# A hybrid mixer with PEER experts: one mixer for all 512 tokens, and U products ahead of the V products

## The chip, the cores and the metric

The kernel runs on one core of a Trainium2 chip. The metric is device microseconds of one execution. Engines: TensorE (PE; PEld is its weight load), VectorE (DVE), ScalarE (ACT), GpSimd (POOL), and SyncE (SP), which issues most DMAs.

## The reference, cut to what matters

512 tokens of width 1024, and 16 learned meta tokens in front of them that are dropped at the end; one layer:

```python
def hybrid_mixer(hn, w_in, w_gate_up, b_gate_up, sb_norm_g, gla_norm_g, w_out):
    proj = hn @ w_in
    ...
    sb_o = stick_breaking_attention(split_heads(sbq, SB_HEADS), split_heads(sbk, SB_HEADS),
                                    split_heads(sbv, SB_HEADS))
    ...
    return jnp.concatenate([sb_o, gla_o], axis=-1) @ w_out
```

Stick-breaking attention has 8 heads of 64: a query weighs a key by sigmoid(z) times the product of (1 − sigmoid) of the later keys, which is a softplus, a sum over keys from the right, and an exp. Beside it stand 4 heads of gated linear attention (GLA), with a decay per key dimension. x + mixer is normed, and goes through PEER: each of 8 heads picks 16 of 128 × 128 experts by product keys (top 16 of each of two lists of 128 scores, then the top 16 of their sums). The output of a token is the sum over its 128 experts of gate · gelu(x · U[e]) · V[e], where U and V are tables of 16384 × 1024 in fp32 (64 MB each). A last residual and a last norm follow.

## The kernel before, in words

The 512 tokens are four blocks of 128. For blocks 0 to 2 the experts are computed densely: the table is walked in 128 rows of 128 experts. A **U row** loads 128 experts of U (512 KB), splits them into a high and a low fp32r part (`hilo`, uh on ScalarE, ul on VectorE), and multiplies them with the normed tokens xDh, xDl (384 columns) in three passes (`mm3`, L187 to L189), which gives a PSUM tile pj, and gelu of it in SBUF. A **V row** loads 128 experts of V (vf, vh, vl), multiplies the gelu tile with the gates gt (L986), splits that into wh and wl, and adds 18 passes of 512 columns to six PSUM banks acc. The gates come from DRAM: top-k gives each token's experts and gates, and `spread` turns them into a dense matrix (one-hot B on VectorE L872, Am on GpSimd L874, matmul L878, stored as Gd; gt are loads of eight rows of it). Block 3 is computed sparsely: 128 gathers of U rows by indirect DMA from GpSimd (L820), a dot product each on VectorE (gu, L827), then 128 gathers of V rows and as many weighted sums (y, L838).

Before, the mixer runs in two groups. Blocks 0 to 2 and the meta tokens go first, in three-pass products. Then block 3 follows in native fp32 (L209), written as generators that a string interleaves by hand with the top-k and the spreads of blocks 0 to 2 and with a few U rows:

```python
SCHED = "f f f u1 f f t0 c1 f f f f m s0 t1 c2 s1 u1 u1 t2 s2 m c3"
```

Here f and m advance block 3's mixer and its second half, t and c the top-k of a block, s its spread, and u a U row. Then U rows run 23 ahead of the V rows in a ring of 24 SBUF tiles, and the main loop goes over 128 steps, each a U row, a V row, and first a share of block 3's top-k, then 2.35 gathers (`GRATE`). Every engine works through its own instructions in program order.

Of the kernel before, what the change touches and what calls it, by code (L numbers as in the profile page):

```python
# [21 lines left out]
D = 1024  # L22
# [7 lines left out]
WF = 2  # L30
GB = 5

SCT = ("px", "pz", "pz", "px")


ORDER = ("nqaylvorx", "nlvorxqay")

GRATE = 2.35
TRATE = 16


SCHED = "f f f u1 f f t0 c1 f f f f m s0 t1 c2 s1 u1 u1 t2 s2 m c3"
# [11 lines left out]
GROUPS = ((0, 1, 2), (3,))  # L54
DENSE = (0, 1, 2)
GATHER = (3,)
ND = len(DENSE)
TT = 16
TB = ND * 128 // TT
IC = 8  # L60

NATIVE_IN = (False, True)
NATIVE_OUT = (False, True)
NATIVE_PQ = (False, True)


def build(tc, d, out):
# [21 lines left out]
    nbuf = dict(pz=3, po=3)  # L89
# [13 lines left out]
    def pk():  # L103
        return bank("pk")

    A.preload_act_table_set(LNEXP)
    Gd = drp.tile([TB, 128, 128, TT], F32, name="Gd")
    hd = drp.tile([4, 128, D], F32, name="hd")

# [26 lines left out]
    def consts_b():  # L136
        nc.sync.dma_start(wgu, d["wgu"])
        nc.sync.dma_start(bgu, d["bgu"])
        lvf = pp.tile([128, 8, 128], F32, name="kT0")
# [51 lines left out]
    def proj(src, c, jobs, act, native, cols=256, halves=(0, 1)):  # L191


        for half in halves:
            wf = wp.tile([128, 4, 256], F32, name="wf", bufs=WF)
            nc.sync.dma_start(wf[:, :, :cols], src[c, :, half * 4:half * 4 + 4, :cols])
            if not native:
                wh = wp.tile([128, 4, 256], F32R, name="wh", bufs=2)
                wl = wp.tile([128, 4, 256], F32R, name="wl", bufs=2)
                hilo(wh[:, :, :cols], wl[:, :, :cols], wf[:, :, :cols])  # L200
            for (o, kind, w0, w1, t0, t1, fst) in jobs:
                for k in range(4):
                    kt = half * 4 + k
                    a = act(kt, t0, t1)
                    st, sp = kt == 0 and fst, kt == KT - 1
                    if native:
                        w = wf[:, k, w0:w1]
                        l, r = (w, a[0]) if kind == 'f' else (a[0], w)
                        T.matmul(o, l, r, start=st, stop=sp, skip_group_check=True)  # L209
                    else:  # L210
                        w = (wh[:, k, w0:w1], wl[:, k, w0:w1])
                        l, r = (w, a) if kind == 'f' else (a, w)
                        mm3(o, l, r, st, sp)

    def token_jobs(nb, lo, bank_):

        banks, outs, jobs = [], [], []
        for b in range(nb):
            if b % 2 == 0:
                banks.append(bank_())  # L220
            o = banks[-1][:, (b % 2) * 256:(b % 2 + 1) * 256]
            outs.append(o)
            jobs.append((o, 't', 0, 256, lo + b * 128, lo + (b + 1) * 128, b % 2 == 0))
        return banks, outs, jobs

    kTs, vts, oTs, qps = {}, {}, {}, {}
    win = d["w_in"]

    def front(g):

        blks = GROUPS[g]
        nb = len(blks)
        W = nb * 128
        E = NM + W
        c0 = 0 if g == 0 else NM
        nt = E - c0
        nat, nato = NATIVE_IN[g], NATIVE_OUT[g]
        pm_ = pj if g == 0 else pk
        oTh = (pp if g == 0 else wp).tile([128, KT, W], F32 if nato else F32R, name=f"oT{g}h")
        oTl = None if nato else pp.tile([128, KT, W], F32R, name=f"oT{g}l")  # L240
        oTs[g] = oTh, oTl
        es = ExitStack()
        ap = es.enter_context(tc.tile_pool(name=f"a{g}", bufs=1, reuse_waits="tile"))
        sbq = ap.tile([128, 4, W], F32, name="sbq")
        kT = (pp if g == 0 else ap).tile([128, 4, W], F32, name=f"kT{g}")
        vt = (pp if g == 0 else ap).tile([128, nb, 512], F32, name=f"v{g}")
        kTs[g], vts[g] = kT, vt
        hnh = ap.tile([128, KT, E], F32 if nat else F32R, name="hnh")
        hnl = None if nat else ap.tile([128, KT, E], F32R, name="hnl")

        tags = itertools.cycle(("pz", "po"))

        def norm_rows(x, rows):

            sq = wp.tile([128, D], F32, name="wf", bufs=WF)[:rows]
            ss = pp.tile([128, 1], F32, name="ssa", bufs=2)[:rows]
            A.activation(sq, x, AF.Square, accum_out=ss)
            r = rstd(ss, 1, rows, pp, "a")
            V.tensor_scalar(x, x, r, None, op0=OP.mult)

        def columns(x, rows, col, q):

            t = bank(next(tags)) if g == 0 else pm_()
            for k in range(4):
                T.transpose(t[:, k * rows:(k + 1) * rows], x[:, (4 * q + k) * 128:(4 * q + k + 1) * 128],
                            ident[:rows, :rows])
            for k in range(4):
                kt = 4 * q + k
                hi = hnh[:, kt, col:col + rows]
                A.activation(hi, t[:, k * rows:(k + 1) * rows], AF.Copy, scale=g1[:, kt:kt + 1])  # L270
                if not nat:
                    V.scalar_tensor_tensor(hnl[:, kt, col:col + rows], t[:, k * rows:(k + 1) * rows],
                                           g1[:, kt:kt + 1], hi.bitcast(F32), op0=OP.mult, op1=OP.subtract)

        def act(kt, a, b):
            return hnh[:, kt, a:b], None if nat else hnl[:, kt, a:b]

        def feat(c, lo):
            n = E - lo
            if 2 * n <= 512:  # L280
                p = pm_()
                outs = [p[:, :n], p[:, n:2 * n]]
            else:
                outs = [pm_()[:, :n] for _ in range(2)]
            proj(win, c, [(outs[m], 'f', m * 128, (m + 1) * 128, lo, E, m == 0 or 2 * n > 512) for m in range(2)],
                 act, nat)
            return outs

        def rows_(c, vtile, mtile):

            banks, outs, jobs = token_jobs(nb, NM, pm_)
            if g == 0:
                pm = banks[-1][:66, 256:]
                jobs.append((pm, 't', 0, 256, 0, 66, False))
            proj(win, c, jobs, act, nat)
            for b in range(0, nb, 2):
                n = min(2, nb - b)
                A.activation(vtile[:, b:b + n], banks[b // 2][:, :n * 256].rearrange("p (b c) -> p b c", b=n), AF.Copy)
            if g == 0:
                A.activation(mtile, pm[:NM], AF.Copy)  # L300

        es2 = es.enter_context(ExitStack())
        gpool = es2.enter_context(tc.tile_pool(name=f"g{g}", bufs=1, reuse_waits="tile"))
        spool = None
        if g == 0:
            spool = es.enter_context(tc.tile_pool(name=f"s{g}", bufs=1, reuse_waits="tile"))
# [5 lines left out]
        gvm = gpool.tile([NM, 512], F32, name="gvm") if g == 0 else None  # L312
        gv = gpool.tile([128, nb, 512], F32, name="gv")
        go = [gpool.tile([128, 2, nb, 128], F32, name=f"go{s}") for s in range(2)]
        gr = gpool.tile([128, 4, W], F32, name="gr")
        rbc, rgk = bc[:, :, NM:], gk[:, :, NM:]
        items = [(pr, b) for pr in range(2) for b in range(nb)]
        ch = nb if nb > 2 else 2 * nb
        pO = []
        def gla_scores():  # L320

            p = pm_()
            proj(win, 12, [(p[:66, :nt], 'f', 0, 66, c0, E, True)], act, nat, cols=66)
            A.activation(glr[:, c0:], p[:16, :nt], AF.Copy)
            for pr in range(2):
                p = pm_()
                T.matmul(p[:, :nt], wgu[:, pr * 128:(pr + 1) * 128], glr[:, c0:], start=True, stop=True)
                y = gpool.tile([128, E], F32, name="dd", bufs=2)[:, :nt]
                V.tensor_scalar(y, p[:, :nt], bgu[:, pr:pr + 1], None, op0=OP.add)
                e = gpool.tile([128, E], F32, name="qk", bufs=2)[:, :nt]  # L330
# [4 lines left out]
                cuts = ([0] if g == 0 else []) + [NM + b * 128 for b in range(nb + 1)]  # L335
                for a, b in zip(cuts[:-1], cuts[1:]):
                    V.tensor_tensor_scan(bc[:, pr, a:b], y[:, a - c0:b - c0], y[:, a - c0:b - c0], 0.0,
                                         op0=OP.add, op1=OP.bypass)

            for m, p in enumerate(feat(6, NM)):  # L340
                A.activation(gq[:, m], p, AF.Copy, scale=0.125)
            for m, p in enumerate(feat(7, c0)):
                A.activation(gk[:, m, c0:], p, AF.Copy)


            for s in range(2):
                P.memset(att[s], 0.0)

            def level(l):


                if l == 7:
                    lq, rq = rgk, gq
                else:
                    H = 1 << l
# [780 lines left out]
```

## Time and profile before

| | |
|---|---|
| time, median of 3 runs | 1720.82 us (1720.75 to 1726.9) |
| profiled execution, own time | 1722.37 us |
| its span | 1720.6 us |
| PE busy | 1608.3 us (93%) |
| DVE busy | 1233.7 us (72%) |
| ACT busy | 704.0 us (41%) |
| POOL busy | 518.2 us (30%) |
| DMA | 376.04 MB, mean 219 GB/s |

Busy times are sums over the span. A busy PE need not be at its peak, since matmuls are pipelined and their ends are modelled: the spacing of their starts is the better price. Idle time of an engine that nobody waits for costs nothing.

### The profile page before, as it was taken

Reading aid. Unit: us, or ns where it says so; the run is one execution under the profiler, and the core shown is the slowest. Engines: PE = TensorE matmul, PEld = TensorE weight load, DVE = VectorE, ACT = ScalarE, POOL = GpSimd, SP = SyncE. Lnnn points to the kernel's source line nnn. Section 1 sums busy time; section 2 is a strip of 40 time slices with the busy share of each in tenths; the row PEclk is TensorE's granted clock in tenths of the full one; section 3 lists DMA queues with packets and bytes.
Section 4 is the critical chain, followed back from the end, with each engine's and each line's share of the span. In section 5 each row is a group of like instructions: output and inputs, shape, how many; then the busy total and the mean of one; then the engine's idle time right before and its main releaser. Section 6 shows DMA issues by size and latency. Waiting matters only on the chain.

```text
span 1720.6 us, 24532 instructions
## 1 busy us (share of the span) xinstructions
PE 1608.3 (93%) x9025; PEld 1432.2 (83%) x9025; DVE 1233.7 (72%) x2484; ACT 704.0 (41%) x1104; POOL 518.2 (30%) x401
## 2 busy tenths in 40 slices
PE   6998998977888789899999999999999999999996
PEld 6957988965577788899999999999999999999875
DVE  4225747489989888978777777777777777777664
ACT  5366365314445456333333333333333333333343
POOL 0020000003345455025334344343444433444310
PEclk9999999999899899999999999999999999999998
DMA  5202125342164345689887887987888888877654
GB/s 172 81 25 86 50 80 172 110 157 102 69 233 165 123 172 203 201 274 369 308 302 283 309 308 281 317 296 289 306 301 292 303 296 299 307 280 279 210 198 133
DMA packets 145705, 376.04 MB, mean 219 GB/s; under 512 B 13712, under 2 KB 63008, under 8 KB 142512
## 3 DMA queue, kind: packets, MB, share of 16 engines
q1 hardware_dynamic: 104112, 211.92, 37.1%
q0 software_dynamic: 36864, 134.23, 21.3%
q10 hardware_dynamic: 4608, 28.31, 4.1%
q8 instruction: 71, 1.16, 0.3%
q14 instruction: 50, 0.41, 0.1%
HBM read 345.03 MB, written 29.36 MB: 218 GB/s over the span
## 4 chain that ended last, share of the span: by engine, by line
PE 79%; DVE 13%; DMA 5%; ACT 2%; issue 1%; POOL 0%; SPq 0%; DVEq 0%; ACTq 0%; POOLq 0%
PE pj L187 12%; PE pj L189 12%; PE pj L188 12%; PE acc L188 9%; PE acc L189 9%; PE acc L187 9%; PE px L878 3%; DVE B L872 2%; PE pk L209 2%; PE pz L373 1%; PE pz L539 1%; DMA vf<-expert_v 1%; PE pz L525 1%; DVE sc L788 1%; DMA wf<-w_out 1%
## 5 line engine op out<-in xcount | busy, mean ns | idle before, releaser
L189 PE MATMUL pj<-xDh,ul 128*128 128x384 f32 x1000 | 338.5, 338 | 5.9 <-DVE ul L183 5.9
L188 PE MATMUL pj<-xDl,uh 128*128 128x384 f32 x1000 | 337.9, 338 | 0.0
L187 PE MATMUL pj<-xDh,uh 128*128 128x384 f32 x1000 | 337.8, 338 | 0.0
L188 PE MATMUL acc<-vl,wh 128*128 128x512 f32 x762 | 298.7, 392 | 1.5 <-DVE vl L183 1.5
L189 PE MATMUL acc<-vh,wl 128*128 128x512 f32 x762 | 298.6, 392 | 0.0
L187 PE MATMUL acc<-vh,wh 128*128 128x512 f32 x762 | 296.3, 389 | 0.4 <-ACT vh L182 0.4
L820 POOL DMA_INDIRECT gu<-expert_u,idx x128 | 183.2, 1431 | 334.4 <-DVE gu L827 193.0
L820 POOL DMA_INDIRECT gu<-expert_v,idx x128 | 178.1, 1392 | 279.3 <-DVE y L838 203.6
L182 ACT ACTIVATE uh<-uf 128x1024 fp32r<-128x1024 f32 x125 | 132.6, 1061 | 300.2 <-PE pj L188 253.6
L874 POOL TENSOR_TENSOR Am<-ohu,ohl 128x512 f32<-128x512 f32 x96 | 129.3, 1367 | 257.0 <-PE pz L530 152.4
L183 DVE TENSOR_TENSOR ul<-uf,uh 128x1024 fp32r<-128x1024 f32 x125 | 157.9, 1263 | 56.2 <-ACT uh L182 56.2
L189 PEld LDWEIGHTS pj<-xDh,ul 128*128 128x128 f32 x1000 | 189.3, 189 | 8.3 <-DVE ul L183 8.1
L187 PEld LDWEIGHTS pj<-xDh,uh 128*128 128x128 f32 x1000 | 189.1, 189 | 4.4 <-ACT uh L182 0.2
L188 PEld LDWEIGHTS pj<-xDl,uh 128*128 128x128 f32 x1000 | 189.3, 189 | 4.1
L188 PEld LDWEIGHTS acc<-vl,wh 128*128 128x128 f32 x762 | 143.0, 188 | 30.6 <-DVE vl L183 2.7
L189 PEld LDWEIGHTS acc<-vh,wl 128*128 128x128 f32 x762 | 143.0, 188 | 29.8
L187 PEld LDWEIGHTS acc<-vh,wh 128*128 128x128 f32 x762 | 143.0, 188 | 28.6 <-ACT vh L182 1.2
L838 DVE SCALAR_TENSOR_TENSOR y<-gu,act,y 128x1024 f32<-128x1024 f32 x128 | 163.8, 1279 | 0.5
L183 DVE TENSOR_TENSOR vl<-vf,vh 128x1024 fp32r<-128x1024 f32 x127 | 154.9, 1220 | 11.2 <-ACT vh L182 11.2
L827 DVE SCALAR_TENSOR_TENSOR gu<-gu,xn 128x1024 f32<-128x1024 f32 x128 | 154.6, 1218 | 0.0
L182 ACT ACTIVATE vh<-vf 128x1024 fp32r<-128x1024 f32 x127 | 133.1, 1048 | 21.1 <-DMA vf<-expert_v 19.8
L878 PE MATMUL px<-Am,B 128*128 128x128 f32 x768 | 102.7, 283 | 26.7 <-DVE B L872 17.1
(365 smaller groups left out, 2458.2 us busy)
## 6 DMA issues: line engine op xcount, KB each, us to landing
vf<-expert_v SPq DMA_DIRECT2D x128, 512.0 KB
uf<-expert_ut SPq DMA_DIRECT2D x125, 512.0 KB
wf<-w_in SPq DMA_DIRECT2D x48, 512.0 KB
Gd<-st ACTq DMA_DIRECT2D x24, 1024.0 KB
gt<-Gd SPq DMA_DIRECT2D x16, 1536.0 KB
wf<-w_out SPq DMA_DIRECT2D x16, 512.0 KB
wf<-w_pq SPq DMA_DIRECT2D x16, 512.0 KB
h<-x SPq DMA_DIRECT2D x4, 512.0 KB
```

The costliest lines, as they stand in the source:

```text
L182: A.activation(hi, src, AF.Copy)
L183: V.tensor_tensor(lo, src, hi.bitcast(F32), op=OP.subtract)
L187: T.matmul(outp, lh, rh, start=first, stop=False, skip_group_check=True)
L188: T.matmul(outp, lh, rl, start=False, stop=False, skip_group_check=True)
L189: T.matmul(outp, ll, rh, start=False, stop=last, skip_group_check=True)
L209: T.matmul(o, l, r, start=st, stop=sp, skip_group_check=True)
L820: P.indirect_dma_start(out=u, out_offset=None, in_=d[table], in_offset=bass.IndirectOffsetOnAxis(ap=col, axis=0))
L827: V.scalar_tensor_tensor(u, u, 1.0, xns[blk], op0=OP.mult, op1=OP.mult, accum_out=acts[blk][:, k:k + 1]))
L838: V.scalar_tensor_tensor(y, u, acts[blk][:, k:k + 1], y, op0=OP.mult, op1=OP.add))
L872: V.tensor_tensor(B, io4, iT[:, 1, c_].unsqueeze(2).to_broadcast(sh), op=OP.is_equal)
L874: P.tensor_tensor(Am.rearrange("p t (u l) -> p t u l", l=8), ohu[:, l_].unsqueeze(3).to_broadcast([128, 4, 16, 8]), ohl[:, l_].unsqueeze(2 ...
L878: T.matmul(p[:, j * 128:(j + 1) * 128], B[:, j], Am[:, j], start=True, stop=True)
```

## The change

One `front` and one `mid` now serve all 512 tokens in three-pass products, with 512 moving columns. The meta tokens get matmuls of their own with 16 columns. Attention is a pipeline of three functions, with scores two steps ahead of the sums:

```diff
+        scores(0)
+        scores(1)
+        for n in range(len(steps)):
+            sticks(n)
+            if n + 2 < len(steps):
+                scores(n + 2)
+            values(n)
```

The hand-written string, the ring and the steps' rates are gone. A `Queue` runs generators by estimated costs (the number that each yield hands over): behind each U row, 4.2 × 1.3 us of top-k and spread work. U rows run in pairs, and 23 pairs are stored to DRAM (Ad) from ScalarE's queue. All top-ks and spreads end before the first V product.

```diff
-GRATE = 2.35
-TRATE = 16
...
-SCHED = "f f f u1 f f t0 c1 f f f f m s0 t1 c2 s1 u1 u1 t2 s2 m c3"
...
+WF = 3
+GB = 6
+GEB = 5
+UF = 4
...
+RATES = (1.3, 0.62)
...
+    def u_row(i1, dst):
+
+        uf = du.tile([128, KT, 128], F32, name="uf", bufs=UF)
+        uh = du.tile([128, KT, 128], F32R, name="uh", bufs=2)
+        ul = du.tile([128, KT, 128], F32R, name="ul", bufs=2)
         nc.sync.dma_start(uf, d["expert_ut"][i1])
         hilo(uh, ul, uf)
...
+    look = Queue(tks[0], spread(0), tks[1], spread(1), tks[2], spread(2), tks[3])
+    np_ = 0
+    while look.jobs and np_ < NK // 2:
+        gp = pair()
+        for i in range(2):
+            u_row(2 * np_ + i, gp[:, i])
+            look.run(4.2 * RATES[0])
+        nc.scalar.dma_start(Ad[np_], gp)
+        np_ += 1
+    look.run(1e9)
```

The dense stage takes the later 41 pairs first: their U rows are computed one pair ahead and used at once. The 23 stored pairs are read back last. Gathers of block 3 run behind U and V rows at 0.62 of the rows' time, 1.3 us counted for each, so about two per row, and are at an end after 125 U and V rows. U and V rows share the buffers uf (four), uh and ul (two each); the gathered rows have six buffers where they had five.

```diff
+    order = list(range(np_, NK // 2)) + list(range(np_))
+    pairs = {}
+
+    def fetch(p_):
+        gp = pairs[p_] = pair()
+        if p_ >= np_:
+            for i in range(2):
+                u_row(2 * p_ + i, gp[:, i])
+                rows.run(4.2 * RATES[1])
         else:
...
+            nc.sync.dma_start(gp, Ad[p_])
```

What stands on VectorE when the first top-k begins, before. The top-k's instructions (MATCH_REPLACE and MAX of sc and vv) stand among the mask copies and products of block 3's GLA (att, qk):

```order
264 L378 COPY_PREDICATED att_2855<-lvm,pz 128x256
265 L378 COPY_PREDICATED att_2856<-lvm,pz 128x256
266 L365 TENSOR_TENSOR qk<-dd,gk 128x2x64
267 L366 TENSOR_TENSOR qk<-dd,gq 128x2x64
268 L747 MATCH_REPLACE sc<-vv,sc 128x128
269 L749 MAX vv<-sc 128x8
270 L378 COPY_PREDICATED att_2855<-lvm,pz 128x256
271 L378 COPY_PREDICATED att_2856<-lvm,pz 128x256
272 L749 MAX vv<-sc 128x8 x5
```

The same place now; ul is the split of a U row:

```order
246 L638 MAX vv<-sc 128x8 x8
247 L175 TENSOR_TENSOR ul<-uf,uh 128x1024
248 L638 MAX vv<-sc 128x8 x8
249 L640 MAX_INDEX iu<-vv,sc 128x8 x8
250 L175 TENSOR_TENSOR ul<-uf,uh 128x1024
251 L640 MAX_INDEX iu<-vv,sc 128x8 x8
252 L642 MATCH_REPLACE sc<-vv,sc 128x128 x16
253 L644 MAX vv<-sc 128x8 x4
254 L175 TENSOR_TENSOR ul<-uf,uh 128x1024
```

Block 3's mixer went ahead, and a split of a U row stands after each 16 to 20 of the top-k's instructions.

The end of block 3's top-k on VectorE and the first gathered rows, now (idx are the experts' numbers, gu a gathered row and its dot, ge a gelu tile times its gates):

```order
601 L702 SCALAR_TENSOR_TENSOR idx_7052<-sel_6679 128x128
602 L175 TENSOR_TENSOR ul<-uf,uh 128x1024
603 L722 SCALAR_TENSOR_TENSOR gu,act_96<-gu,xn_3217 128x1024 x3
604 L175 TENSOR_TENSOR ul<-uf,uh 128x1024
605 L722 SCALAR_TENSOR_TENSOR gu,act_96<-gu,xn_3217 128x1024 x2
606 L841 TENSOR_TENSOR ge<-ge,gt 128x384
607 L722 SCALAR_TENSOR_TENSOR gu,act_96<-gu,xn_3217 128x1024
608 L175 TENSOR_TENSOR wl_7248<-ge,wh_7247 128x384
```

Five dots of gathered rows stand ahead of the operand of the first V row.

In the middle of the gathered V rows, VectorE before (y are the weighted sums of block 3):

```order
902 L838 SCALAR_TENSOR_TENSOR y<-gu,act_93,y 128x1024
903 L183 TENSOR_TENSOR vl<-vf,vh 128x1024
904 L838 SCALAR_TENSOR_TENSOR y<-gu,act_93,y 128x1024
905 L183 TENSOR_TENSOR ul<-uf,uh 128x1024
906 L986 TENSOR_TENSOR oT0h<-oT0h,gt 128x384
907 L183 TENSOR_TENSOR wl_8808<-v_5838,wh_8807 128x384
908 L838 SCALAR_TENSOR_TENSOR y<-gu,act_93,y 128x1024
909 L183 TENSOR_TENSOR vl<-vf,vh 128x1024
910 L838 SCALAR_TENSOR_TENSOR y<-gu,act_93,y 128x1024
```

And now:

```order
653 L733 SCALAR_TENSOR_TENSOR y<-gu,act_96,y 128x1024
654 L175 TENSOR_TENSOR wl_7839<-ge,wh_7838 128x384
655 L175 TENSOR_TENSOR ul<-uf,uh 128x1024
656 L733 SCALAR_TENSOR_TENSOR y<-gu,act_96,y 128x1024 x2
657 L175 TENSOR_TENSOR wl_7874<-ge,wh_7873 128x384
658 L175 TENSOR_TENSOR ul<-uf,uh 128x1024
659 L733 SCALAR_TENSOR_TENSOR y<-gu,act_96,y 128x1024 x3
660 L175 TENSOR_TENSOR ul<-uf,uh 128x1024
661 L733 SCALAR_TENSOR_TENSOR y<-gu,act_96,y 128x1024
```

Where one y stood per split of 1024 columns (vl or ul), about two stand now.

## Rows read from the trace of the kernel before

**Rows 1.** The page: the chain that ended last, by engine.

```profile
PE 79%; DVE 13%; DMA 5%; ACT 2%; issue 1%; POOL 0%; SPq 0%; DVEq 0%; ACTq 0%; POOLq 0%
```

**Rows 2.** Windows by stage: us, busy PE, PEld, DVE, ACT, POOL, clock, DMA, GB/s.

```profile
0.00:82.00 82.00, 67.07 (x416) 65.31 (x416) 29.29 (x72) 34.72 (x82) 2.76 (x13) 1.00 0.43 133
82.00:141.00 59.00, 58.60 (x305) 34.51 (x304) 11.96 (x18) 35.87 (x68) 13.51 (x26) 1.00 0.07 23
141.00:242.00 101.00, 96.17 (x684) 85.83 (x683) 61.20 (x116) 50.25 (x89) 0.31 (x1) 0.97 0.21 71
242.00:294.00 52.00, 46.41 (x358) 42.59 (x357) 37.32 (x69) 33.01 (x70) 0.31 (x1) 0.97 0.53 177
294.00:328.00 34.00, 34.00 (x199) 34.00 (x200) 9.81 (x13) 12.59 (x23) 0.00 (x0) 1.00 0.18 62
328.00:737.00 409.00, 338.45 (x2250) 299.05 (x2249) 369.37 (x1283) 188.43 (x278) 139.96 (x104) 0.96 0.45 157
737.00:1600.00 863.00, 863.00 (x4366) 785.80 (x4365) 641.57 (x814) 303.61 (x423) 344.66 (x244) 1.00 0.86 300
1600.00:1720.60 120.60, 104.65 (x460) 85.14 (x458) 73.18 (x102) 45.53 (x74) 16.68 (x12) 0.96 0.54 178
```

**Rows 3.** Timeline of PE, a row's first matmul each: start, us, instruction.

```profile
80.05 0.28 PE L188 MATMUL pj<-wl,hnh 128*128 128x256 f32 x1
80.17 0.28 PE L189 MATMUL pj<-wh,hnl 128*128 128x256 f32 x1
...
1002.48 0.33 PE L187 MATMUL pj<-xDh,uh 128*128 128x384 f32 x1
...
1006.66 0.39 PE L187 MATMUL acc<-vh,wh 128*128 128x512 f32 x1
...
1010.78 0.33 PE L187 MATMUL pj<-xDh,uh 128*128 128x384 f32 x1
```

**Rows 4.** Groups by line, 328 to 737 us: busy, mean ns, idle before.

```profile
L872 DVE TENSOR_TENSOR B<-io,iT 128x512 f32<-128x512 f32 x96 | 88.5, 935 | 11.4 <-PE px L878 11.2
L183 DVE TENSOR_TENSOR ul<-uf,uh 128x1024 fp32r<-128x1024 f32 x21 | 30.6, 1459 | 2.7 <-ACT uh L182 2.7
L378 DVE COPY_PREDICATED att<-lvm,pz 128x256 f32<-128x256 uint8 x16 | 6.2, 438 | 0.2
L183 DVE TENSOR_TENSOR oT0l<-kT,oT0l 128x1024 fp32r<-128x1024 f32 x3 | 3.6, 1208 | 0.0
L878 PE MATMUL px<-Am,B 128*128 128x128 f32 x768 | 102.7, 283 | 26.7 <-DVE B L872 17.1 <-issue 5.6 <-POOL Am L874 3.3
```

**Rows 5.** Timeline of DVE in the dense stage.

```profile
774.95 1.22 DVE L183 TENSOR_TENSOR ul<-uf,uh 128x1024 fp32r<-128x1024 f32 x1
776.09 0.55 DVE L986 TENSOR_TENSOR oT0h<-oT0h,gt 128x384 f32<-128x384 f32 x1
...
777.03 1.22 DVE L827 SCALAR_TENSOR_TENSOR gu<-gu,xn 128x1024 f32<-128x1024 f32 x1
...
778.17 1.22 DVE L183 TENSOR_TENSOR vl<-vf,vh 128x1024 fp32r<-128x1024 f32 x1
...
1105.55 2.60 DVE L838 SCALAR_TENSOR_TENSOR y<-gu,act,y 128x1024 f32<-128x1024 f32 x2
```

**Rows 6.** Windows in a top-k and in spreads, columns as in rows 2.

```profile
360.00:400.00 40.00, 27.92 (x213) 24.66 (x209) 38.85 (x222) 10.69 (x34) 0.00 (x0) 1.00 0.48 161
540.00:680.00 140.00, 117.14 (x823) 111.13 (x822) 123.72 (x263) 78.56 (x91) 80.45 (x59) 0.95 0.44 165
```

**Rows 7.** Timeline of POOL: gathers, idle before and its releaser in brackets.

```profile
747.39 1.10 POOL L820 DMA_INDIRECT gu<-expert_u,idx  x1 [0.31 <-issue]
...
780.81 1.68 POOL L820 DMA_INDIRECT gu<-expert_u,idx  x1 [0.60 <-DVE gu L827]
```

**Rows 8.** Windows in the first gathers, columns as in rows 2.

```profile
760.00:800.00 40.00, 40.00 (x205) 36.58 (x204) 36.34 (x56) 14.37 (x20) 18.31 (x12) 1.00 1.06 371
780.00:790.00 10.00, 10.00 (x54) 9.26 (x53) 7.67 (x13) 2.55 (x4) 4.45 (x5) 1.00 1.03 409
```

More of the change, by code (lines that the diff above doesn't have):

```diff
@@ L204, in proj @@
                     a = act(kt, t0, t1)
[L205 to L213, printed above, removed]
@@ new lines, in proj, with token_jobs @@
+                    w = (wh[:, k, w0:w1], wl[:, k, w0:w1])
+                    l, r = (w, a) if kind == 'f' else (a, w)
+                    mm3(o, l, r, kt == 0 and fst, kt == KT - 1)
+    def token_jobs(lo, banks):
+        return [(banks[b // 2][:, (b % 2) * 256:(b % 2 + 1) * 256], 't', 0, 256, lo + b * 128, lo + (b + 1) * 128,
+                 b % 2 == 0) for b in range(NB)]
+    win = d["w_in"]
+    oTh = wp.tile([128, KT, W], F32R, name="oTh")
+    oTl = wp.tile([128, KT, W], F32R, name="oTl")
@@ L257, in norm_rows @@
             A.activation(sq, x, AF.Square, accum_out=ss)
-            r = rstd(ss, 1, rows, pp, "a")
+            r = rstd(ss, 1, n, pp, "a")
             V.tensor_scalar(x, x, r, None, op0=OP.mult)
[L261 to L273, printed above, removed]
@@ L275, in act @@
-        def act(kt, a, b):
[L276 to L286, printed above, removed]
+        tags = itertools.cycle(("pz", "po", "po"))
@@ L287, in feat @@
+        consts_b()
+        def act(kt, a, b):
+            return hnh[:, kt, a:b], hnl[:, kt, a:b]
+        def feat(c, meta=None):
+            outs = [pj(), pj()]
+            jobs = [(outs[m], 'f', m * 128, (m + 1) * 128, NM, E, True) for m in range(2)]
+            if meta is not None:
+                jobs += [(meta[:, m * 16:(m + 1) * 16], 'f', m * 128, (m + 1) * 128, 0, NM, m == 0) for m in range(2)]
+            proj(win, c, jobs, act)
             return outs
         def rows_(c, vtile, mtile):
-            banks, outs, jobs = token_jobs(nb, NM, pm_)
@@ L292, in rows_ @@
[L292 to L303, printed above, removed]
@@ new lines, in values @@
+        def values(n):
+            kb, nq, nh, pr0 = steps[n]
+            for i in range(nh):
+                pr = pr0 + i
+                for b in range(kb, NB):
+                    cb_ = i * nq + (b - kb) * 128
+                    for s in range(2):
+                        hh = 2 * pr + s
+                        T.matmul(pO[b][s * 64:(s + 1) * 64, pr * 128:(pr + 1) * 128],
+                                 vt[:, kb, hh * 64:(hh + 1) * 64], as_[n][s][:, cb_:cb_ + 128],
+                                 start=(b == kb and pr == 0), stop=False, skip_group_check=True)
@@ new lines, in front @@
+        scores(0)
[5 more added lines that the diff above has]
+            values(n)
+        z = pz()
+        for pr in range(4):
+            T.matmul(z[pr * 32:(pr + 1) * 32], kbd[:, pr, :], sbq[:, pr, :], start=True, stop=False,
+                     skip_group_check=True)
+        sp = spool.tile([128, 512], F32, name="sp", bufs=4)
+        softplus(z, W, sp)
+        for hh in range(NH):
+            pr, s = divmod(hh, 2)
+            T.matmul(z, csel[:, 112 - 16 * hh:240 - 16 * hh], RS[:, s, pr], start=False, stop=False,
+                     skip_group_check=True)
@@ new lines, in front @@
+        T.matmul(z, negTb, sp, start=False, stop=True, skip_group_check=True)
+        a = spool.tile([128, 512], F32, name="a", bufs=4)
+        A.activation(a, z, AF.Exp)
+        for b in range(NB):
+            for pr in range(4):
+                T.matmul(pO[b][:, pr * 128:(pr + 1) * 128], vbd[:, pr, :], a[:, b * 128:(b + 1) * 128],
+                         start=False, stop=True, skip_group_check=True)
+        es1.close()
+        gpool = es.enter_context(tc.tile_pool(name="gla", bufs=1, reuse_waits="tile"))
@@ new lines, in build, with __init__, run @@
+    bp = pool_open("bld", "bld")
+    class Queue:
+        def __init__(self, *jobs):
+            self.jobs, self.owed = list(jobs), 0.0
+        def run(self, us):
+            self.owed += us
+            while self.jobs and self.owed > 0:
+                c = next(self.jobs[0], None)
+                if c is None:
+                    self.jobs.pop(0)
+                else:
+                    self.owed -= c
+            if not self.jobs:
+                self.owed = 0.0
+    tks = {b: topk(b) for b in range(NB)}
@@ L1025, in build @@
[L1025 to L1044 removed]
+    gen = gathered(GATHER[0])
@@ new lines, in build @@
+    rows = Queue(gen)
+    order = list(range(np_, NK // 2)) + list(range(np_))
[3 more added lines that the diff above has]
+        if p_ >= np_:
+            for i in range(2):
+                u_row(2 * p_ + i, gp[:, i])
+                rows.run(4.2 * RATES[1])
+        else:
+            nc.sync.dma_start(gp, Ad[p_])
+    left = []
+    fetch(order[0])
+    for n, p_ in enumerate(order):
+        if n + 1 < NK // 2:
+            fetch(order[n + 1])
+        gp = pairs.pop(p_)
+        for i in range(2):
+            ops = v_operands(2 * p_ + i, gp[:, i])
+            if n < NK // 2 - 1:
+                for b in range(ND):
+                    for j in range(2):
+                        v_block(ops, b, j, n == 0 and i == 0, False)
+            else:
+                left.append(ops)
+            rows.run(4.1 * RATES[1])
```

858 lines of the change are left out of this document (332 added, 526 removed).

## The prediction

> **What bounds the kernel now.** I read the chain of waits first: TensorE holds most of it, VectorE a seventh [rows 1]. Then the windows by stage [rows 2]. Up to 328 us (projections, attention, gated linear attention, output projection, norm and query projection of blocks 0 to 2) TensorE is busy nearly throughout. From 328 to 737 it is busy for 338 of 409 us and VectorE for 369: here the top-k of four blocks, three spreads, the mixer of block 3 and 23 U rows stand together, and VectorE is the fuller engine. From 737 to 1600 TensorE never pauses, VectorE has a quarter of its time free, and the DMA engines move 300 GB/s. The reader should see in [rows 2] that TensorE is the limit of every stage but one, and that the change works on both kinds: it takes TensorE work out of the mixer of block 3, and it puts U rows where VectorE is the limit.
>
> **The mixer of 512 tokens, priced stage by stage.** On TensorE the spacing of starts is the price: passes of 256 columns of a three-pass product start 0.12 us apart, a U row (24 passes of 384 columns) takes 1006.66 − 1002.48 = 4.18 us, a V row (18 passes of 512) 1010.78 − 1006.66 = 4.12, so 0.229 for 512 columns [rows 3].
> - Start and attention projections, 82 us now. The q and k chunks become 192 passes of 512 columns (44.0 us), the v chunks 240 of 256 columns (28.6), and 96 passes of the 16 meta columns are new. No row shows one so narrow: it costs between 0 and the 0.12 of 256 columns. I take 0.08, 8 us (0 to 11). With 3 us of start that is 84 where 60 stood, and 3.5 for a fourth block in the first norm: 109.5.
> - Attention, 59 now. Its score columns go from 6,144 to 10,240, which at the present cost per column is 98. But the present stretch has VectorE and ScalarE partly idle and TensorE's weight loads at 34 of 59 [rows 2]; in between, TensorE waits for softplus inside what is modelled as busy. The change issues scores two steps ahead, so that this wait has other matmuls in it. Without any gain it is 98, with all of the waits gone I estimate 70; I take 79.
> - Gated linear attention, 101 now: four thirds is 135; the meta state and the constants don't grow; 130.
> - Output projection and second norm, 52 now: 96 more passes of 256 columns (11.4) and a fourth block's norm and transposes (4 to 5): 68.
> - Query projection, 34 now: 192 passes of 512 columns, 44.
>
> Together 430.5 where 328 stood, bounds 415 to 455. All of block 3's native-fp32 work in 328 to 737 is removed for it.
>
> **The look stage.** Four top-ks and three spreads are now alone with 50 U rows (46 stored, the others the first used at once). VectorE's need: 369 us in the stage of before, and the last 5 us of block 3's top-k, which lie just behind it. Off go the pieces of block 3's mixer (the largest are 16 mask copies of 0.44 us [rows 4]; the some twenty groups together about 22), 24 splits of U rows (21 of 1.46 and 3 of 1.21 us [rows 4], less overlap, 33), and V operands of the first five V rows (6). That leaves 313. On come 50 splits at 1.14 us, their spacing where nothing disturbs them [rows 5], to 1.46 as in this stage: 57 to 73, I take 64. Sum 377. How full does VectorE get? 97% in a stretch of pure top-k, 88% in one of spreads [rows 6], where B waits for the matmuls that read it (11 us before B [rows 4]). With U rows between, a spread's matmuls queue behind 4.18 us of U row on TensorE in order, but the spread has three buffers and six PSUM banks. I take 96%: 393, with 378 (98%, cheap splits) and 415 (93%) as ends, and 3 for the first scores. TensorE needs 50 × 4.18 + 103 for the spreads' matmuls [rows 4] + 10, so 322, and is no bound; its 70 idle us remain idle. The stores of 23 pairs of 393 KB on ScalarE's queue stand behind the Gelu that fills them, and the DMA engines are under half busy here [rows 2]: nothing, unless this cover goes, and then at most 9 MB, some 25 us.
>
> **The start of the V products.** Before, U rows covered the arrival of the first gathers. Now the first ge × gt stands behind five dots of gathered rows on VectorE, and these behind idx. A gather is issued every 1.4 us at best [rows 7]; five take 7, and the landing a few more, while two U rows still run. I take 8 (0 to 15).
>
> **The gather stretch.** 256 gathers and their dots and sums stand beside 62 U and 63 V rows, where the kernel before spread them over 863 us. For this stretch:
> - TensorE: 62 × 4.18 + 63 × 4.12 = 519.
> - VectorE: 125 splits × 1.14, 128 dots × 1.14, 128 sums × 1.30, 64 pairs of ge × gt and its split × 0.94 [rows 5]: 143 + 146 + 166 + 60 = 515 (99% of TensorE's).
> - GpSimd: 256 gathers at 1.4, issued freely, to 2.3, when a dot must free the buffer [rows 7]: 358 to 589.
> - DMA: 125 rows and 256 gathers of 524 KB each, and eight gt of 1.57 MB, make 212 MB. In the busiest 40 us of before 371 GB/s came with the engines' share over 1, in ten of them 409 [rows 8]: 571 to 518.
>
> Four resources at 515 to 550 can't be packed without gaps: a wait of one is a wait of all, since V products need ge × gt from an in-order VectorE that stands behind dots, which stand behind gathers, and the loads of U and V rows share one queue and four buffers with gt behind them. I take 390 GB/s, the middle of the two rows: 543 (518 to 590). For the transfers the Trainium skill has a rule that speaks against this change: "DMA: Bandwidth & Descriptors", section "Where 436 GB/s comes from", says that between HBM and SBUF the HBM side's share of about 358 GB/s binds, not the port's 435. By it 212 MB would take 593 us and the sum would be 50 us longer. The 371 and 409 GB/s of [rows 8] are already above it, so that I don't take it.
>
> **The rest.** 16 U and 65 V rows at TensorE's pace, 335, with reading back 23 pairs (9 MB in 300 us, hidden). The end behind the last product is as before, 15 us.
>
> **Sum.** 430.5 + 396 + 8 + 543 + 335 + 15 = 1727.5 us. The sum is made against the profiled execution, whose span was 1720.6 and own time 1722.4; the median of the runs is 1720.8, equal to the span. I forecast 1727.
>
> **The rivals.**
> - A: the gather stretch keeps TensorE's pace. For it: between 760 and 800 us TensorE was busy for 40 of 40 us, with VectorE at 36 and the DMA engines at 371 GB/s [rows 8]. Against: that demand lasted 40 us. Then the stretch is 519, the time 1703. It decides at a V and U row's VectorE work, with its waits, under 8.3 us.
> - C: the mixer and the look stage pack better: attention 70 and VectorE at 98% with cheap splits, 378. −9 and −15: 1703. For it the 97% of the pure top-k [rows 6]; against, the spreads' 88%. With A, 1679.
> - B, the other side, slower: the transfers bound the gather stretch at the 371 GB/s that 40 us have shown, or GpSimd does at 2.3 us per gather. 571 to 589 makes 1756 to 1773. It decides when the DMA engines sustain less than 385 GB/s. For it: gt comes in pieces of 512 bytes and all loads collide; against: 409 in ten us. The skill's rule above would end here too.
> - D, slower: attention goes by columns (98, +19), or VectorE is as full as in the whole present stage, 90% (419, +26): 1746 to 1753.
> - That the change doesn't do what it says, so that the U rows ahead don't fit beside the look, hardly can be: TensorE has 70 us free there.
>
> **How the numbers follow.** A measurement of this kernel tells about 0.5% from no change, 1712 to 1729. Forecast (1712 to 1745): 0.36, of it 0.04 faster, 0.17 same, 0.15 slower. A 0.20, A with C 0.03, C 0.14, all faster. B 0.16 and D 0.09, slower. The other 0.02 I count as same. So 0.41 faster, 0.19 same, 0.40 slower. The range, 1680 to 1768, goes from A with C nearly to the far end of B; the forecast's own is 1712 to 1745.
>
> **What would show it.** V products' first matmul should start near 835 us (430 + 396 + 8). The window from there to the last gather's sum should last 543 us with VectorE over 92% busy and the DMA engines near 390 GB/s; 519 with TensorE never idle is A, 570 or more with the DMA share at 1 is B. Attention of 70, 79 or 98 us and VectorE's share in the look stage decide C and D. I am wrong altogether if the last 81 rows run slower than TensorE's pace, since I see nothing there to hold them.

## The result, and the profile after

The changed kernel takes 1915.25 us (median of 4 runs, 1910.73 to 1921.35) where the kernel before takes 1720.78: a ratio of 1.113, with a 95% interval of 1.108 to 1.117. It is 11% slower, and 147 us above the end of the range. The profiled execution took 1921.35 us, its span is 1919.5.

The windows of the changed kernel by stage: us, busy time of PE, PEld, DVE, ACT and POOL, granted clock, DMA share, GB/s.

```profile
0.00:120.00 120.00, 101.61 (x569) 87.90 (x570) 32.97 (x86) 40.30 (x96) 1.46 (x11) 0.96 0.31 99
120.00:200.00 80.00, 74.62 (x434) 41.22 (x434) 15.56 (x25) 46.59 (x95) 25.17 (x44) 1.00 0.04 11
200.00:324.00 124.00, 112.96 (x780) 96.31 (x779) 72.01 (x116) 58.79 (x84) 0.00 (x0) 0.94 0.17 54
324.00:404.00 80.00, 69.33 (x531) 62.83 (x531) 43.86 (x80) 39.55 (x79) 0.00 (x0) 0.91 0.31 112
404.00:450.00 46.00, 46.00 (x198) 37.28 (x198) 8.73 (x8) 11.31 (x16) 0.00 (x0) 0.97 0.21 69
450.00:887.00 437.00, 346.22 (x2058) 324.84 (x2057) 382.14 (x1228) 185.58 (x223) 133.30 (x96) 0.92 0.39 140
887.00:907.00 20.00, 10.57 (x54) 9.86 (x53) 11.70 (x19) 4.74 (x7) 13.44 (x12) 0.79 1.06 371
907.00:1552.00 645.00, 562.31 (x2600) 499.39 (x2599) 502.60 (x628) 181.44 (x255) 350.57 (x245) 0.92 0.90 323
1552.00:1905.00 353.00, 344.58 (x1574) 289.08 (x1572) 170.11 (x231) 127.70 (x183) 0.00 (x0) 1.00 0.56 179
```

They answer to [rows 2]. The stages are: start and attention projections, attention, GLA, output projection with norm, query projection, look stage, wait for the first V product, gather stretch, and the rest, with 14.5 us of tail. Against the forecast:

| stage | forecast, us | measured | difference |
|---|---|---|---|
| mixer and query projection (0 to 450) | 430.5 | 450 | +19.5 |
| of it attention | 79 | 80 | +1 |
| scores and look | 396 | 437 | +41 |
| wait for the first V product | 8 | 20 | +12 |
| gather stretch | 543 | 645 | +102 |
| rest | 335 | 353 | +18 |
| tail | 15 | 14.5 | 0 |

Over half of the miss is in the gather stretch. There TensorE is idle for 83 of 645 us, and from its granted clock of 0.92 I estimate that it stood at its lower level, 1.2 GHz, for some 100 us. In [rows 2] the dense stage had neither. What TensorE and VectorE waited for there, with the total, the number of times and the longest:

```profile
PE pj L181 <- DVE ul L175: 40.7, 17, 5.0
PE pj L179 <- ACT uh L174: 35.1, 7, 6.7
```

```profile
DVE ul L175 <- ACT uh L174: 66.1, 29, 8.5
DVE gu L722 <- DMA gu<-expert_u,idx: 56.1, 18, 5.4
```

One of these waits, in the timeline of the changed kernel: ScalarE waits 6.7 us for a U row's load, then TensorE starts again.

```profile
1163.13 1.06 ACT L174 ACTIVATE uh<-uf 128x1024 fp32r<-128x1024 f32 x1 [6.70 <-DMA uf<-expert_ut]
```

```profile
1159.91 0.39 PE L181 MATMUL acc<-uh,wl 128*128 128x512 f32 x1
1164.24 0.45 PE L179 MATMUL pj<-xDh,uh 128*128 128x384 f32 x1 [3.94 <-ACT uh L174]
...
1166.30 0.52 PE L180 MATMUL pj<-xDl,uh 128*128 128x384 f32 x1
1166.62 0.52 PE L181 MATMUL pj<-xDh,ul 128*128 128x384 f32 x1
...
1171.86 0.34 PE L180 MATMUL pj<-xDl,uh 128*128 128x384 f32 x1
1172.04 0.34 PE L181 MATMUL pj<-xDh,ul 128*128 128x384 f32 x1
```

The reader should see two prices of one late load. TensorE stands still for 3.94 us. Then its matmuls start 0.32 us apart in place of 0.17, until about 1171: the clock has fallen to its lower level (granted clock 0.53 from 1164.3 to 1171.4, 0.99 behind), and so a U row that waited 4 us is 8 us late.

### The profile page after: what moved, and what is told of

Same layout as the page of the kernel before. It is cut to its first block, busy times and chain, and to the rows that moved or that the text cites. A ratio compares the mean times of both kernels' runs of the same rounds, so it can differ in the third digit from the quotient of the medians.

```text
span 1919.5 us, 23858 instructions
## 1 busy us (share of the span) xinstructions
PE 1668.2 (87%) x8783; PEld 1448.7 (75%) x8783; DVE 1246.5 (65%) x2436; ACT 697.8 (36%) x1039; POOL 523.9 (27%) x407
## 4 chain that ended last, share of the span: by engine, by line
PE 44%; DVE 20%; issue 15%; DMA 10%; POOL 6%; ACT 4%; DVEq 0%; SPq 0%; POOLq 0%; ACTq 0%
PE pj L181 7%; PE pj L179 7%; PE pj L180 7%; POOL gu L715 6%; PE acc L180 5%; PE acc L179 5%; PE acc L181 5%; DMA uf<-expert_ut 4%; DVE ul L175 3%; DVE B L769 3%; DMA gu<-expert_v,idx 2%; PE sx L775 2%; DMA gu<-expert_u,idx 2%; DVE y L733 1%; DVE sc L683 1%
## 5 line engine op out<-in xcount | busy, mean ns | idle before, releaser
L174 ACT ACTIVATE uh<-uf 128x1024 fp32r<-128x1024 f32 x256 | 269.6, 1053 | 509.3 <-PE pj L180 391.2
L175 DVE TENSOR_TENSOR ul<-uf,uh 128x1024 fp32r<-128x1024 f32 x256 | 321.3, 1255 | 146.1 <-ACT uh L174 143.2
L179 PE MATMUL acc<-uh,wh 128*128 128x512 f32 x768 | 303.9, 396 | 11.0 <-ACT wh L174 11.0
L180 PE MATMUL acc<-ul,wh 128*128 128x512 f32 x768 | 305.0, 397 | 4.0 <-DVE ul L175 4.0
L181 PE MATMUL acc<-uh,wl 128*128 128x512 f32 x768 | 303.8, 396 | 0.4 <-DVE wl L175 0.4
L174 ACT ACTIVATE wh<-ge 128x384 fp32r<-128x384 f32 x128 | 67.0, 524 | 320.7 <-PE acc L180 271.4
L179 PEld LDWEIGHTS acc<-uh,wh 128*128 128x128 f32 x768 | 144.6, 188 | 45.6 <-ACT wh L174 11.9
L180 PEld LDWEIGHTS acc<-ul,wh 128*128 128x128 f32 x768 | 144.6, 188 | 40.1 <-DVE ul L175 6.9
L181 PEld LDWEIGHTS acc<-uh,wl 128*128 128x128 f32 x768 | 144.5, 188 | 35.5 <-DVE wl L175 1.1
L775 PE MATMUL sx<-Am,B 128*128 128x128 f32 x768 | 105.7, 289 | 30.2 <-DVE B L769 25.1
```

The costliest lines, as they stand in the source:

```text
L174: A.activation(hi, src, AF.Copy)
L175: V.tensor_tensor(lo, src, hi.bitcast(F32), op=OP.subtract)
L179: T.matmul(outp, lh, rh, start=first, stop=False, skip_group_check=True)
L180: T.matmul(outp, lh, rl, start=False, stop=False, skip_group_check=True)
L181: T.matmul(outp, ll, rh, start=False, stop=last, skip_group_check=True)
L775: T.matmul(p[:, j * 128:(j + 1) * 128], B[:, j], Am[:, j], start=True, stop=True)
```

## The experiments

Two theories stood at first. S: the gather stretch is too full, its transfers above all. P: U and V rows in pairs, with shared operand buffers, hold each other up, gathers or not. Times given without an interval are of one execution, or the median of two.

**Gathers spread out, left out, and halved in two ways.** Four changes to the changed kernel:

```diff
-RATES = (1.3, 0.62)
+RATES = (1.3, 0.40)
```

> Gathers at 0.40 of the rows' time, 1.3 per row over some 198 of the 210 U and V rows, in place of 2 per row over 125. Theory S (too much in one stretch: with two gathers per row the transfers and VectorE's in-order queue are too full, each wait of TensorE is made longer by its fallen clock): the dense stage, 1033 us from idx to the end, loses most of its 110 us of waits, and the kernel takes 1800 to 1840. Rival P (the waits come from U and V rows in pairs that share two uh, two ul and four uf buffers, gathers or not): 1890 to 1920.

Without gathers, dots and sums:

```diff
                 for k in range(hh * TK, (hh + 1) * TK):
-                    u_dot(blk, k)
                     yield 1.3
-                weights(blk, slice(hh * TK, (hh + 1) * TK))
...
                 for k in range((hh - 1) * TK, hh * TK):
-                    v_sum(blk, y, k)
                     yield 1.3
```

> Leaves out block 3's experts: no gather, no dot, no weighted sum. S: the dense stage runs at TensorE's pace, 82 U rows of 4.18 and 128 V rows of 4.12, 870 us and some 25 of start and end: the kernel takes about 1780. P: at least 60 us of TensorE's waits stay: 1850 or more. What it takes over 1780 is no cost of the gathers.

Gathers with thin dots:

```diff
-            V.scalar_tensor_tensor(u, u, 1.0, xns[blk], op0=OP.mult, op1=OP.mult, accum_out=acts[blk][:, k:k + 1]))
+            V.scalar_tensor_tensor(u[:, :64], u[:, :64], 1.0, xns[blk][:, :64], op0=OP.mult, op1=OP.mult,
+                                   accum_out=acts[blk][:, k:k + 1]))
...
-            V.scalar_tensor_tensor(y, u, acts[blk][:, k:k + 1], y, op0=OP.mult, op1=OP.add))
+            V.scalar_tensor_tensor(y[:, :64], u[:, :64], acts[blk][:, k:k + 1], y[:, :64], op0=OP.mult, op1=OP.add))
```

> All 256 gathers, but dots and sums over 64 of 1024 columns (so block 3 is computed in part): some 285 us less on VectorE, the same transfers. If the transfers set the stretch (212 MB at 359 GB/s per busy DMA engine time is 590 us), the stretch from the first V product to the last sum stays at 590 to 645 and the kernel over 1850. If VectorE's queue sets it, it falls to 520 to 540: 1800.

Dots without gathers:

```diff
-        u = gather("expert_u", idxs[blk][:, k:k + 1])
+        u = gb.tile([128, D], F32, name="gu", bufs=GB)
...
-            V.scalar_tensor_tensor(u, u, 1.0, xns[blk], op0=OP.mult, op1=OP.mult, accum_out=acts[blk][:, k:k + 1]))
+            V.scalar_tensor_tensor(u, xns[blk], 1.0, xns[blk], op0=OP.mult, op1=OP.mult, accum_out=acts[blk][:, k:k + 1]))
...
-        u = gather("expert_v", idxs[blk][:, k:k + 1])
+        u = xns[blk]
```

> All 256 dots and sums over 1024 columns, but on data already in SBUF, without gathers (so block 3's experts are not computed): VectorE as before, 134 MB fewer transfers, no GpSimd. If the transfers set the stretch: 520 to 540 us, the kernel at about 1800. If VectorE's queue does: 600 to 645, over 1850.

Measured: 1839.56 us at 0.40 (ratio 1.070, 1.066 to 1.075), 1782.21 without gathers, 1877.89 with thin dots, 1793.76 with dots but no gathers. The windows of the four, in this order of kernels: thin dots over its gather stretch, dots without gathers over the same rows, and the middle of the run at 0.40.

```profile
907.00:1500.00 593.00, 532.60 (x2540) 469.30 (x2539) 258.82 (x616) 178.13 (x251) 262.94 (x243) 0.96 0.95 349
```

```profile
907.00:1424.00 517.00, 517.00 (x2597) 466.60 (x2597) 497.09 (x622) 180.61 (x255) 0.00 (x0) 1.00 0.45 149
```

```profile
970.00:1570.00 600.00, 600.00 (x3017) 541.74 (x3016) 461.50 (x565) 209.41 (x292) 250.65 (x183) 1.00 0.88 309
```

With VectorE 96% busy and no gathers, TensorE never waits: 517 us for nearly the same number of matmuls that took 645. So VectorE's queue alone is no limit. With the gathers and VectorE less than half busy, the stretch still takes 593 us, with the DMA engines busy for 0.95 of it. So the gathers set it, through their transfers as I read it, and both together add 52 us more. GpSimd's issuing of the gathers into six buffers is not taken apart from the transfers by this run. At 0.40 the middle runs at TensorE's pace with 309 GB/s. P falls in the form that it had: without gathers the dense stage has 8 us of idle TensorE between 887 and 1766. The gathers' cost is 1915 − 1782 = 133 us at 0.62 and 57 at 0.40; of the 57, part lies behind 1570, where stored pairs are read back.

**Where the demand passes what the engines can move, and the bursts.** Five more changes to the changed kernel: only the first load of gt kept (later rows then use the first rows' gates); gathers at 0.52; U and V rows in turn; seven gather buffers; three uh and ul buffers.

```diff
+            if gt is None:
...
-RATES = (1.3, 0.62)
+RATES = (1.3, 0.52)
...
+            if n + 1 < NK // 2:
+                fetch(order[n + 1], (i,))
...
-GB = 6
+GB = 7
...
-        ul = du.tile([128, KT, 128], F32R, name="ul", bufs=2)
+        ul = du.tile([128, KT, 128], F32R, name="ul", bufs=3)
```

> The changed kernel (0.62) with only the first load of gt, so wrong gates in later rows: 12.6 MB in pieces of 512 bytes less in the gather stretch, 200 MB left. If bytes at 359 GB/s of busy time set the stretch: 35 us shorter, about 1880. If the small pieces cost what their time in the records says (the engines moved 290 instead of 410 GB/s beside them): 50 to 70 us shorter, 1845 to 1865. If the gathers alone set it: no change.

> Gathers at 0.52 of the rows' time, 1.68 per row over some 153 rows: 365 GB/s asked for at TensorE's pace, about the 359 that the busy DMA engines gave at 0.62. If the loss starts where the demand passes some 360 GB/s: the stretch is at most 2 to 5% over TensorE's pace, and the kernel between 0.45 and 0.62 but near the former: 1820 to 1850. If it grows with every gather: (1840 + 1915) / 2, about 1875.

> The changed kernel (0.62) with U and V rows in turn (U, V, U, V) in place of pairs (U, U, V, V). With thin dots the transfers alone took 593 us for the gather stretch, with no gathers VectorE alone 521, and both 645: some 52 us come from both together. If they come from loads that go out in pairs (bursts, then nothing): about 600 for the stretch, 1870 for the kernel. If from any in-order wait of a dot for its gather: 640, 1910.

> The changed kernel with seven buffers for gathered rows in place of six. If the 52 us come from dots that wait for gathers issued too late (57 us of VectorE's waits): 10 to 30 us less. If the transfers are full whenever they can be: within 10 us of 1915, or longer, since one more gather in flight delays the loads of U and V rows.

> The changed kernel with three uh and three ul buffers in place of two, so that a row's operands can be split while the row before is waited for. If the 52 us come from too short a lead of the operands: 20 to 50 us less. If not: within 10 us of 1915.

Measured: 1870.25, 1843.32, 1863.09, 1890.24 and 1852.98 us. The windows of the gather stretch with rows in turn, and with three operand buffers:

```profile
907.00:1493.00 586.00, 544.92 (x2612) 484.80 (x2611) 502.06 (x632) 184.16 (x257) 343.77 (x246) 0.96 0.98 358
```

```profile
907.00:1490.00 583.00, 526.98 (x2542) 468.48 (x2541) 487.17 (x614) 178.63 (x252) 348.12 (x240) 0.95 0.96 351
```

In the changed kernel the DMA engines were busy for 0.90 of the stretch at 323 GB/s. Either edit closes the gaps: 0.96 to 0.98 busy, 351 to 358 GB/s, the stretch some 60 us shorter. Each by itself ends at the length that the run with thin dots took. So I read two parts in the loss: 583 to 593 us is about what 212 MB of this mix need, and the 52 to 62 on top come from gaps in the transfers, which loads that go out in pairs and operands that are split late leave open. This is a part of P that holds, but only under a full load. With seven gather buffers 25 us come back, and dots still wait 41 us for gathered U rows; so gathers that are issued late have a share in the gaps too. The three edits overlap, and no two of them were run together at 0.62, so that 583 us is not shown to be a floor. GpSimd at 2.3 us per gather, the other half of rival B, would give 589. Against it: with rows in turn VectorE waits only 13 us for gathered rows, and taking gt's loads away, with all 256 gathers left, makes the kernel faster. Without gt's later loads 45 us come back, between the two expectations, more than their 12.6 MB need at 358 GB/s (35). At 0.52 the kernel is as fast as at 0.40, but for two reasons that cancel: between 907 and 1552 us TensorE is idle for 7 us at 0.40, 10 at 0.45 (the run of the next group), 30 at 0.52 and 83 at 0.62, while at 0.40 gathers are left that stand beside the read-back, and from 1552 to the tail TensorE idles for 34 us, at 0.52 for 12. So the loss in this stretch sets in between 0.45 and 0.52, where 325 and 365 GB/s are asked for.

**U rows ahead.** Three runs on the look stage and the read-back:

```diff
-RATES = (1.3, 0.62)
+RATES = (1.3, 0.45)
...
+        while nf < NK // 2 and nf <= n + (1 if order[nf] >= np_ else 3):
+            fetch(order[nf])
+            nf += 1
```

> Gathers at 0.45 of the rows' time (1.45 per row, over some 177 rows), and the stored pairs read back up to three pairs ahead in place of one. At 0.40 the middle of the dense stage ran at TensorE's pace with 310 GB/s, and VectorE waited 49 us for stored pairs. If only transfers over some 359 GB/s and late read-back cost time: this asks for 325 GB/s, so no waits in the middle and none of the 40 us behind it, 1795 to 1810. If the gathers disturb at any rate: 1830 or more.

```diff
-RATES = (1.3, 0.62)
+RATES = (2.6, 0.40)
```

> Twice the look work behind each U row, so some 24 U rows ahead in place of 46; gathers at 0.40 as in the first run. If the look stage is bound by VectorE's own work, a U row there costs its split and a little waiting, 1.3 to 2.5 us: the look stage gets 30 to 55 us shorter, the dense stage 90 longer, 1875 to 1900 against 1840. If U rows and spreads hold each other up in TensorE's and VectorE's order, a U row in the look stage costs 4.2 us or more, and the time is 1840 or less.

```diff
-            look.run(4.2 * RATES[0])
+            look.run(1e9)
```

> All look work right behind the first U row, none beside later ones; gathers at 0.40. The look stage is then the price of top-k and spreads alone: VectorE's 313 us at 88 to 97% full is 323 to 355. The dense stage has nearly all U rows, 44 more than in the first run at 4.18: 1840 − 437 + 323 to 355 + 185 makes 1910 to 1945.

Measured: 1825.86, 1827.08 and 1894.23 us. The look stage with 26 splits of U rows, and with 8:

```profile
450.00:832.00 382.00, 260.93 (x1520) 238.70 (x1519) 358.10 (x1204) 156.69 (x177) 129.67 (x96) 0.84 0.31 118
```

```profile
450.00:807.00 357.00, 159.70 (x1063) 143.72 (x1061) 338.20 (x1187) 126.32 (x138) 126.74 (x96) 0.75 0.23 89
```

The first 18 rows cost 25 us, 1.4 each, a split's time. The next 23, up to the 49 of the changed kernel, cost 55, 2.4 each. There VectorE waits for the others: 28.5 us before B and 16.5 before ul, where it waits 4.7 and 0 with 26 splits and 0.2 and 0 with 8. In the changed kernel:

```profile
DVE B L769 <- PE sx L775: 28.5, 17, 4.7
DVE ul L175 <- ACT uh L174: 16.5, 6, 5.9
DVE vv L638 <- ACT sc L626: 14.0, 3, 10.6
```

My expectation for 24 rows (1875 to 1900) missed: it took the dense stage to pay 4.2 us for each row moved back, some 90 us, and it got 45 longer. TensorE's idle time there fell from 50 us to 14. The likely reason, not tested by itself, is that 23 more U rows give the gathers more rows to stand beside, and leave fewer pairs to read back. So the time fell where the other branch of the expectation had it, but not by its reason: a U row in the look stage cost 2.4 us and not 4.2.

The read-back three pairs ahead gave less than expected. I had aimed at the 49 us that VectorE waits for stored pairs at 0.40, and 43 are left. But that sum is no price: without any gather VectorE waits 42 us for stored pairs too, at most 3.1 at a time, and TensorE never waits. Beside gathers single waits reach 9 us; I take it that these reach TensorE, and not the sum.

**Block 3's mixer in the kernel before.** The changed kernel without any gather is still 62 us above before. In the kernel before, the string was changed so that block 3's mixer comes first:

```diff
-SCHED = "f f f u1 f f t0 c1 f f f f m s0 t1 c2 s1 u1 u1 t2 s2 m c3"
+SCHED = "f f f f f f f f f f f f m m u1 t0 c1 s0 t1 c2 s1 u1 u1 t2 s2 c3"
```

> The kernel before, with one string changed: all of block 3's native mixer first, then the top-ks and spreads of blocks 0 to 2 that it was interleaved with; nothing else. If that mixer's TensorE work lay free beside VectorE's (the look stage of before: VectorE 369 of 409 us), taking it out costs its own length, 130 us of TensorE and waits, less the 22 us of VectorE that go with it: 1800 to 1840. If it was paid for there anyway: 1720 to 1740, and the change's loss before the dense stage has another cause.

1735.05 us, a ratio of 1.0095 (1.0066 to 1.0125). The run does not answer the question: the instructions of the two stayed mixed on the engines, with the first MAX of the top-k at 332 us as before, and block 3's projections until 519. Then with a dependence that forces the order:

```diff
+        if blk == 0:
+            for s in range(2):
+                V.tensor_copy(sc[:, s, :, 0:1], qps[1][:, :, 0:1])
```

> The kernel before with the string of the last such run and two copies of 16 numbers that make the first top-k wait for block 3's queries. In the last run the scheduler put the top-k's instructions among block 3's mixer as before, so that it moved little (1735). If that mixer's TensorE work lay free beside VectorE's top-k and spreads: its own length, 130 us or more as it is a chain of small steps, less the 22 us of VectorE: 1800 to 1870. If it was paid for there anyway: under 1750.

1821.19 us, a ratio of 1.0595 (1.056 to 1.063): 102 us slower. Here block 3's last projection ends at 509 us and the first MAX starts at 510.7. Its mixer of block 3, with five splits of U rows in it, and its look stage:

```profile
328.00:510.00 182.00, 151.76 (x976) 123.85 (x975) 37.51 (x87) 58.14 (x123) 8.82 (x8) 0.97 0.41 142
510.00:840.00 330.00, 226.35 (x1361) 208.80 (x1360) 318.56 (x1177) 146.80 (x165) 124.84 (x96) 0.85 0.33 120
```

Together 512 us, where the kernel before takes 409 [rows 2]. So of the 182 us that block 3's mixer takes by itself, some 102 lay free beside VectorE's work in the kernel before, and some 80 did not.

**Together.** Rows in turn, three operand buffers, gathers at 0.45, and read-back ahead; then the same with 2.0 in place of 1.3.

```diff
+            if n + 1 < NK // 2 and order[n + 1] >= np_:
+                fetch(order[n + 1], (i,))
+            for q in order[n + 1:n + 4]:
+                if i == 0 and q < np_ and q not in pairs:
+                    fetch(q)
...
-RATES = (1.3, 0.62)
+RATES = (1.3, 0.45)
```

> The changed kernel with what was found: U and V rows in turn, three uh and ul buffers, gathers at 0.45, stored pairs read back up to three pairs ahead. The dense stage should then run at TensorE's pace: the 1782 without gathers, less some 10 that a faster look stage gave with three operand buffers, and 10 for the start: 1775 to 1795. If over 1810, gathers cost something that neither rate nor buffers touch.

> The same with 2.0 for the look work per U row, some 32 U rows ahead in place of 46. By the runs with 24 and with none ahead a U row in the look stage costs 1.1 us at first and 2.4 beyond 24, always under the 4.2 that it saves: 20 to 40 us longer than with 1.3. If the look stage's waits come mainly from U rows, equal or shorter.

1794.81 and 1817.73 us, ratios 1.044 and 1.058 to the kernel before. The first gives back 120 of the 194 us. In the second 16 fewer U rows stand in the look stage, which is 27 us shorter, and the kernel is 23 us longer. No version tried is below the kernel before.

## Why the prediction was wrong

**The gather stretch was mis-sized (+102 us), and this alone would have put the time out of the range.** The step that failed is "I take 390 GB/s, the middle of the two rows". The rows [rows 8] were of 40 and 10 us, at the start of the gathers, and I took their rate for one that lasts. Over 580 us the engines moved 351 to 358 GB/s when they were busy for 0.96 to 0.98, and that makes the 543 of the sum some 583 to 593. The rule of the Trainium skill that I set aside ("DMA: Bandwidth & Descriptors", section "Where 436 GB/s comes from") gives 593 us by its 358 GB/s for 212 MB, an estimate. The traces agree with it in the mean: the run with thin dots took 593, and that with rows in turn 586 at 358 GB/s. Shorter stretches went above it, 386 GB/s over 100 us with thin dots (900 to 1000) and 369 over 200 with three operand buffers (1000 to 1200), so that it is not shown as a limit at every moment. That the transfers bound the stretch was rival B, at 0.16, with 571; with its other half, GpSimd, up to 589. The 52 to 62 us more I had named ("a wait of one is a wait of all"), but the sum has no term for them: 543 is 212 MB at 390 GB/s and nothing else.

**Rival A fell, but its number held for VectorE.** TensorE and VectorE alone took 517 us for this stretch (forecast 519), with VectorE 96% busy. What A lacked was the gathers' transfers.

**I left out the clock.** No term of the sum held it. At a clock of 0.92, the gather stretch's matmuls were busy for 562 us where 517 do: 45 us, beside 83 of idle time. The look stage had the same 0.92, against 0.96 in [rows 2]. The wait shown above, 3.94 us, cost as much again in matmuls that started 0.32 us apart.

**The look stage (+41): fullness, more than work.** The sum of VectorE's work was 377 us, measured 382, in part by luck: B took 102 us where it took 88.5 before [rows 4], and other work came out as much shorter. The step that failed is "I take 96%": it was 87%. Rival D had 90%. The run with 8 splits shows 95% (338 of 357); with 26 it is 94%, with 49 it is 87%, and the waits before B grow from 0.2 to 4.7 and 28.5 us. So the U rows themselves, queued on TensorE between the spreads' matmuls, cost this. By these prices a U row ahead saves 4.2 − 2.4 = 1.8 us and not 2.9. Whether that is got depends on the dense stage: in the last pair of runs 16 rows fewer cost 23 us, but at 0.40 it was faster by 12 to have 26 rows ahead than 49.

**The mixer (+19.5).** Attention came out as chosen (80 for 79, between bounds of 70 and 98 that no row narrowed), and GLA was shorter (124 for 130). The start took 10 us more, and output projection with norm 12 more; in both the clock fell. In the latter, TensorE is busy for 62 of 66 us at a granted clock of 1.00, and then for 7 of 14, from 390 to 404, at 0.50. The 16-column matmuls of the meta tokens cost the upper end of my bounds, as their rows show:

```profile
70.76 0.26 PE L180 MATMUL pz<-hnl,wh 128*128 128x16 f32 x1
70.87 0.26 PE L181 MATMUL pz<-hnh,wl 128*128 128x16 f32 x1
...
73.62 0.63 PE L179 MATMUL pj<-hnh,wh 128*128 128x512 f32 x1
74.05 0.63 PE L180 MATMUL pj<-hnl,wh 128*128 128x512 f32 x1
```

They start 0.11 us apart, nearly as 256 columns do (0.12 [rows 3]). Shortly behind 24 of them, from 72.8 to 75.8, matmuls of 512 columns start 0.43 us apart in place of 0.23. The page "TensorE: Matmul & The Clock Gate" of the Trainium skill, section "LDWEIGHTS (loading the stationary operand)", has a weight load's time go with the 128 columns of the stationary operand; an estimate by its figure is 0.107 us, which the rows agree with. That narrow matmuls made the clock fall was not tested.

**The sum of stages did not show what the change gives up.** It was the right sum, but reading it I did not say how much of block 3's mixer had been free. The forced run shows it: 102 of 182 us. With gathers and their losses left out, the changed kernel is at 1782, which fits this: it takes 122 us more than before up to the look stage and 28 more in it, and 90 less behind it. TensorE's work did not shrink by the measure of its busy time: up to the end of the look stage it is busy for 641 us before and 751 now, and without U rows, 24 and 49 at 4.18, I estimate about 540 and 546, at a lower clock now. And it is idle for more: 46 us in place of 26 before the look stage, 91 in place of 71 in it.

**The wait for the first V product (+12) and the rest (+18)** were mis-sized too. Ge × gt stood behind five dots, and the first of them started at 895.9 us, 10 behind idx, at a DMA share of 1.06, where I had given the gathers a few us. In the rest, 1574 matmuls fell after the last sum where I counted 1554, and TensorE was idle for 8 us.

What stays open: whether rows in turn and three operand buffers together would take the gather stretch at 0.62 below 583 us, and what makes stored pairs late beside gathers even when they are asked for three pairs ahead. Without gathers they cost TensorE nothing, as the run without them and the end of the changed kernel show (0.3 us of waits from 1552 to 1905).

## What to carry to other kernels

Take a transfer rate for a stretch from a stretch of the same length: 371 GB/s over 40 us was not had over 600 in any run here. When two streams of work are made denser, count the stretch's bytes against the rate first, then ask what idles when a load is late, since TensorE paid twice for its waits, 83 us of idle time and 45 of slower matmuls. And before a block of TensorE work is moved out of a stage that VectorE limits, force it out in the old kernel and take the time: here that cost 102 us, less than the block takes by itself, but more than nothing.

## What the runs showed that I had not expected

- VectorE 96% busy over 517 us, in program order, with 1.8 us of TensorE's waits in all.
- 351 to 358 GB/s as the most that any run moved over 580 us of loads of 512 KB, gathered rows of 4 KB and pieces of 512 bytes together, though 200 us reach 369 and 10 us 409 [rows 8].
- Matmuls of 16 columns cost 0.11 us, nearly as much as those of 256 (0.12).
- One more pair of operand buffers (two to three) was worth 62 us where the DMA engines were 0.90 busy.
